# Latent attention's output projection and memory attention worked in two halves of the tokens

## The chip, the cores and the metric

The kernel runs on one core of a Trainium2 chip. The metric is the device time of one execution in microseconds (us). TensorE (PE in the rows) does the matmuls, VectorE (DVE), ScalarE (ACT) and GpSimd (POOL) do the rest, and SyncE (SP) issues the loads.

## The reference, cut to what matters

A first block is followed by two layers of a second block, for 512 tokens of width 1024. In each layer x is the residual stream:

```
x = x + 0.5 * swiglu(rms_norm(x, ffn1_norm), ...)
... three mixers: latent attention, windowed attention, neighbourhood attention
x = x + concat(rms_norm(o_mla), rms_norm(o_swa), rms_norm(o_na)) @ w_mix_out
h = rms_norm(x, mem_norm_x);  m = rms_norm(mem, mem_norm_m)
q = rms_norm((h @ w_q).reshape(512, 4, 64), q_gain)
k, v = split(m @ w_kv);  k = rms_norm(k.reshape(256, 4, 64), k_gain)
p = softmax(q @ k.T * 64 ** -0.5)      # 512 tokens x 256 memory rows, per head
x = x + (p @ v) @ w_o
x = x + 0.5 * swiglu(rms_norm(x, ffn2_norm), ...)
x = rms_norm(x, block_norm)
```

The change lies in the four lines from the projection of o_mla to w_o, in both layers.

## The kernel before, in words

x is held turned: eight tiles X(0) to X(7) of 128 features by 512 tokens. A weight matrix is loaded raw, and ScalarE and VectorE split it into a high and a low part (`chunk3`, L361 and L362); activations are split likewise (`split`, L371 to L375), and a product takes three matmuls for each 128 rows of contraction: high by high, high by low, low by high (`gemm_f`, L383 to L385, features out; `gemm_t`, L406 to L408, tokens out). There are four pairs of split weight buffers (`p_w`), two raw ones, nine `h` tiles, and in PSUM three `acc`, two `ss` and three `st` banks.

`mixer` ends with `out_proj("mla")` (L1625): for each of the eight d, 12 matmuls of 512 columns into an `ss` bank, then an addition to X(d) (L1634). `memory` (L1687) follows:

- `norm_split` scales and splits each X(k) into x (L374, L375), squares it on ScalarE (L483) and adds the squares up on GpSimd (L488). `norm.cols` sums over the features with one-column matmuls (L429) and takes the root on GpSimd (L420).
- The queries of token tile i are 24 matmuls of 256 columns. `query` (L1700) scales them by the norm (L1702), norms each head (`head_norm`, L1313 to L1316, its root at L420), and `place` (L1695) turns them (L413) and splits them into qT. The `later` and `tick` calls set by how many steps a piece of work is put off.
- `Attn` with `per=2` works in eight items, two heads of one token tile each (heads h and h + 2): `scores` (six matmuls of 64 rows by 256 columns into one `ss` bank, L1133 to L1135; maximum, L1145; exponential, L1148), `turn` (four transposes and a copy, L1183) and `values` (eight matmuls of 64 columns, L1200; division by the sum, L1213). `piped` runs scores two steps ahead of turn and three ahead of values.
- `turned` turns and splits the result, and `out(0)` and `out(1)` project it for tokens 0 to 255 and 256 to 511 (48 matmuls of 256 columns each, additions at L1735). `out(0)` runs in the background of the attention, `out(1)` at the end.

Then `norm_split` and `ffn` for ffn2 begin. The kernel is written in one stream, and every engine's queue is fixed when it is built: the framework (`TileContext(nc, schedule_with_timeline_sim=True)`) goes through the stream with a model of its own, and lets an instruction that it holds ready go ahead of one that it holds waiting. So the order on an engine is near that of the stream, and not the same. On the chip each queue is strictly in order.

Of the kernel before, what the change touches and what calls it, by code (L numbers as in the profile page):

```python
# [8 lines left out]
F32 = mybir.dt.float32  # L9
F32R = mybir.dt.float32r  # L10
# [29 lines left out]
def _chunks(w, width):  # L40
    return np.stack([_ktile(w[:, i:i + width]) for i in range(0, w.shape[1], width)])
# [87 lines left out]
def prep(I):  # L129
# [76 lines left out]
    for l in range(L2):  # L206
        for n in ("ffn1", "ffn2"):
            w = I[f"{n}_w_in_2"][l]
            w = np.concatenate([w[:, :FF].reshape(D, NFF, 128), w[:, FF:].reshape(D, NFF, 128)], axis=2).reshape(D, -1)
            A[f"{n}_a{l}"] = _chunks(w, 256)  # L210
            w = I[f"{n}_w_out_2"][l]
            A[f"{n}_b{l}"] = np.concatenate([_chunks(w[:FF // 2], 128), _chunks(w[FF // 2:], 128)])
        w = I["w_mix_in_2"][l]
        A[f"mixq{l}"] = _ktile(w[:, :256])
        A[f"mixkv{l}"] = _ktile(w[:, 256:384])
        sq = w[:, 416:672].reshape(D, 4, 64)[:, [0, 2, 1, 3]].reshape(D, 256)
        za = np.concatenate([w[:, 384:416], sq, w[:, 672:928]], axis=1)
# [9 lines left out]
        A[f"memq{l}"] = _chunks(I["mem_w_q_2"][l], 256)  # L227
        A[f"memkv{l}"] = _chunks(I["mem_w_kv_2"][l], 256)
# [9 lines left out]
class Prog:  # L238
# [104 lines left out]
        return self.p_s.tile([128, 32], F32, name="s", tag="s", bufs=17)[:, :n]  # L343


    def chunk3(self, ap, k, parts=1, low=None):

        nc = self.nc
        low = low or nc.vector
        c = ap.shape[1] // k  # L350
        per = k if k * c <= CH // 2 else -(-k // 2)
        hi, lo = [], []
        for k0 in range(0, k, per):
            m = min(per, k - k0) * c
            h = self.p_w.tile([128, CH // 2], F32R, name="wh", tag="wh")
            l = self.p_w.tile([128, CH // 2], F32R, name="wl", tag="wl")
# [149 lines left out]
def nat(i):  # L506
    return lambda t: t[:, i * 128:(i + 1) * 128]
# [24 lines left out]
def v3(t):  # L532
    return t.rearrange("p (h i) -> p h i", h=4)
# [560 lines left out]
class Attn:  # L1094
# [22 lines left out]
    def scores(self, a, b):  # L1117
        g, nc = self.g, self.g.nc
        i, h = self.tile_head(a, b)
        n_in = 4 if self.by_head else self.nh  # L1120
        lo, hi = self.window(i)
        n = hi - lo
        if b == 0:
            self.st[a] = g.small(32)
            self.bt = self.bias(i) if self.bias else None
        m, w, per = self.st[a], n * 128, self.per
        s = g.ss()[:, :per * w]
        for j in range(per):
            sj = s[:, j * w:(j + 1) * w]
            q, k = self.qT(h + j * self.step, i), self.kT(h + j * self.step)  # L1130
            if isinstance(q, tuple):
                k = [t[:, lo * 128:hi * 128] for t in k]
                nc.tensor.matmul(sj, q[0], k[0], start=True, stop=False)  # L1133
                nc.tensor.matmul(sj, q[0], k[1], start=False, stop=False)
                nc.tensor.matmul(sj, q[1], k[0], start=False, stop=True)  # L1135
            else:
                nc.tensor.matmul(v3(sj), q, k[:, lo:hi], start=True, stop=True)
        P = g.p()
        mx, l = (m[:, o + b:o + b + (per - 1) * self.step + 1:self.step] for o in (0, n_in))
        if self.bt:  # L1140
            nc.vector.tensor_tensor_reduce(P[:, :w], s, self.bt(h, lo, hi), -1.0,
                                           self.sink[:, h:h + 1] if self.sink is not None else 3e38, OP.add, OP.min, mx)
            nc.scalar.activation(P[:, :w], P[:, :w], AF.Exp, scale=-1.0, bias=mx, accum_out=l)
        else:
            nc.vector.tensor_reduce(mx, s.rearrange("p (j k) -> p j k", j=per) if per > 1 else s, axis=AX.X, op=OP.max, negate=True)  # L1145
            for j in range(per):
                c = slice(j * w, (j + 1) * w)
                nc.scalar.activation(P[:, c], s[:, c], AF.Exp, bias=mx[:, j:j + 1], accum_out=l[:, j:j + 1])  # L1148
        self.st[a, b] = P

    def scores2(self, i, h0, h1):
# [236 lines left out]
def mixer(g, l, xt, c2):  # L1388
# [298 lines left out]
def memory(g, l, xt, mem):  # L1687
    nc, A = g.nc, g.A
    X = tview(xt)
    norm = g.norm_split(X, g.c(f"mem_norm_x{l}"))  # L1690
    wh, wl = g.chunk3(A[f"memq{l}"][0], 8)
    qT = g.h(F32R)
    gq = gain_col(g, "mem", l, 0.125)

    def place(i, z):  # L1695
        ps = g.st()
# [3 lines left out]
    def query(i, ps):  # L1700
        z = g.b()[:, :256]
        nc.scalar.activation(z, ps[:, :256], AF.Copy, scale=norm.cols()[:, i:i + 1])  # L1702
        head_norm(g, z, 4, 64)
        g.later(2, place, i, z)


    pss = [g.acc() for i in range(3)]
    for ks in (range(6), range(6, KD)):
        for i in range(3):
            g.gemm_t(pss[i][:, :256], norm.parts, nat(i), wh, wl, 0, 256, ks)  # L1710
            if ks[-1] == KD - 1:
                query(i, pss[i])
                g.tick()
    half = lambda t, hb: t[hb * 64:hb * 64 + 64]
    o = g.h()
    hi, lo = g.h(F32R), g.h(F32R)
    w = {}

    def turned(i):
        ps = g.st()  # L1720
        g.turn(ps, lambda c: o[:, i, hs(c)], 2)
        kv = ps[:, :256].rearrange("p (k t) -> p k t", k=2)
        g.split(kv, hi[:, 0:2, hs(i)], lo[:, 0:2, hs(i)])
        if i == 1:
            g.bg.append(out(0))

    def out(hf):
        if not w:
            w["o"] = g.chunk3(A[f"memo{l}"], 2)
        c = slice(hf * 256, hf * 256 + 256)  # L1730
        parts = [(hi[:, k, c], lo[:, k, c]) for k in range(2)]
        for k in range(KD):
            ps = g.acc()[:, :256]
            g.gemm_f(ps, *w["o"], k * 128, k * 128 + 128, parts)
            nc.vector.tensor_tensor(X(k)[:, c], X(k)[:, c], ps, op=OP.add)  # L1735
            yield

    at = Attn(g, 4, 64, lambda h, i: tuple(half(qT[:, c + h // 2, hs(i)], h % 2) for c in (0, 2)),
              lambda h: [half(t[:, (h // 2) * 256:(h // 2) * 256 + 256], h % 2) for t in mem.kT],
              lambda t, h: mem.v[:, t * 256 + h * 64:t * 256 + h * 64 + 64], lambda i: o[:, i, :256],  # L1740
              lambda i: (0, 2), None, None, lambda i: g.later(1, turned, i), per=2)
    ps = g.ss()
    g.gemm_t(ps[:, :256], norm.parts, nat(3), wh, wl, 0, 256)
    query(3, ps)
    g.tick()
    g.pipe(at.items(), steps=2)
    g.flush()
    for _ in out(1):
        pass
# [38 lines left out]
def second_block(g, xt):  # L1788
# [5 lines left out]
    x, row = norm.parts, norm.row  # L1794
    for l in range(L2):
        ffn(g, "ffn1", l, xt, x, row)
        mem = mixer(g, l, xt, c2)
        memory(g, l, xt, mem)
# [49 lines left out]
```

## Time and profile before

| | us |
|---|---|
| median of 3 runs | 2894.86 |
| lowest and highest of them | 2879.66, 4008.79 |
| profiled execution | 2895.25 |
| its span | 2893.5 |
| TensorE busy in it | 2827.5 |
| VectorE, ScalarE, GpSimd busy | 1458.4, 1162.8, 464.0 |

The profiled execution's time is 1.75 us above its span, and 0.39 us above the median. The highest run stands alone. A matmul's start-to-start distance to the next, and not the duration in its row, says what it takes of TensorE's time, since matmuls overlap.

### The profile page before, as it was taken

How to read it: one execution, taken by the hardware profiler on the slowest of the kernel's cores; microseconds unless marked ns; L12 is line 12 of the kernel's file. 1: busy time of each engine (PE TensorE's matmuls, PEld its weight loads, DVE VectorE, ACT ScalarE, POOL GpSimd, SP SyncE). 2: the span in 40 equal slices, each digit the busy share in tenths (PEclk: the TensorE clock that was granted, in tenths of full speed). 3: DMA queues.
4: the chain of work that ended last, by engine and by line, in shares of the span. 5: the costliest groups of instructions: out<-in, count | busy, mean ns of one | idle time of the engine just before them, and what ended most of it. 6: DMA issues, size and time to landing. Idle time of an engine off the chain costs nothing.

```text
span 2893.5 us, 37993 instructions
## 1 busy us (share of the span) xinstructions
PE 2827.5 (98%) x15101; PEld 2399.4 (83%) x15101; DVE 1458.4 (50%) x2338; ACT 1162.8 (40%) x2008; POOL 464.0 (16%) x557
## 2 busy tenths in 40 slices
PE   8999999999999999999999999999999899999998
PEld 6798999888888888778888888888888778888887
DVE  5734455445434444677643444534444676644442
ACT  5323444533322235765432234322335765332232
POOL 4422222002000013512200003000013512200001
PEclk9999999999999999999799999999999999799999
DMA  4111222233323232212133323233232212133322
GB/s 154 52 45 59 74 73 74 73 103 122 99 87 105 86 106 75 68 37 66 38 102 90 107 88 108 88 85 112 84 107 70 63 40 72 31 102 90 107 88 80
DMA packets 78322, 239.63 MB, mean 83 GB/s; under 512 B 8512, under 2 KB 14656, under 8 KB 78016
## 3 DMA queue, kind: packets, MB, share of 16 engines
q1 hardware_dynamic: 78144, 237.20, 26.0%
q8 instruction: 119, 1.95, 0.3%
q14 instruction: 59, 0.48, 0.1%
HBM read 235.06 MB, written 2.10 MB: 82 GB/s over the span
## 4 chain that ended last, share of the span: by engine, by line
PE 91%; DVE 4%; ACT 2%; POOL 1%; issue 1%; DMA 0%; DVEq 0%; SPq 0%; ACTq 0%; POOLq 0%
PE ss L383 12%; PE ss L384 12%; PE ss L385 12%; PE acc L383 8%; PE acc L385 8%; PE acc L384 8%; PE acc L406 4%; PE acc L408 4%; PE acc L407 4%; PE st L413 3%; PE acc L1200 2%; PE ss L1236 2%; DVE b L611 1%; PE acc L396 1%; PE acc L395 1%; PE acc L397 1%
## 5 line engine op out<-in xcount | busy, mean ns | idle before, releaser
L362 DVE TENSOR_TENSOR wl<-raw,wh 128x1024 fp32r<-128x1024 f32 (+3 forms) x447 | 506.9, 1134 | 558.9 <-ACT wh L361 558.0
L361 ACT ACTIVATE wh<-raw 128x1024 fp32r<-128x1024 f32 (+3 forms) x459 | 449.9, 980 | 731.8 <-PE ss L384 533.7
L383 PE MATMUL acc<-x,wh 128*128 128x512 f32 x1048 | 412.7, 394 | 8.4 <-ACT wh L361 8.1
L385 PE MATMUL acc<-x,wl 128*128 128x512 f32 x1048 | 413.4, 394 | 0.1
L384 PE MATMUL acc<-x,wh 128*128 128x512 f32 x1048 | 411.3, 393 | 0.0
L383 PE MATMUL ss<-h,wh 128*128 128x512 f32 (+1 forms) x843 | 328.7, 390 | 0.0
L385 PE MATMUL ss<-h,wl 128*128 128x512 f32 (+1 forms) x843 | 326.1, 388 | 0.0
L384 PE MATMUL ss<-h,wh 128*128 128x512 f32 (+1 forms) x843 | 326.0, 388 | 0.0
L488 POOL TENSOR_TENSOR b<-b 128x512 f32<-128x512 f32 (+1 forms) x77 | 106.6, 1385 | 1176.6 <-ACT b L483 1068.6
L383 PE MATMUL ss<-x,wh 128*128 128x512 f32 x672 | 261.5, 389 | 0.1
L385 PE MATMUL ss<-x,wl 128*128 128x512 f32 x672 | 261.4, 389 | 0.0
L384 PE MATMUL ss<-x,wh 128*128 128x512 f32 x672 | 261.4, 389 | 0.0
L406 PE MATMUL acc<-wh,x 128*128 128x256 f32 (+1 forms) x880 | 252.8, 288 | 0.0
L407 PE MATMUL acc<-wl,x 128*128 128x256 f32 (+1 forms) x880 | 252.6, 288 | 0.0
L383 PEld LDWEIGHTS acc<-x,wh 128*128 128x128 f32 x1048 | 198.1, 189 | 50.8 <-ACT wh L361 8.5
L385 PEld LDWEIGHTS acc<-x,wl 128*128 128x128 f32 x1048 | 197.9, 189 | 42.6 <-DVE wl L362 1.6
L408 PE MATMUL acc<-wh,x 128*128 128x256 f32 (+1 forms) x816 | 232.1, 286 | 0.0
L384 PEld LDWEIGHTS acc<-x,wh 128*128 128x128 f32 x1048 | 197.9, 189 | 41.1 <-DVE x L375 0.6
L383 PEld LDWEIGHTS ss<-h,wh 128*128 128x128 f32 x843 | 159.3, 189 | 33.1 <-issue 0.6
L385 PEld LDWEIGHTS ss<-h,wl 128*128 128x128 f32 x843 | 159.5, 189 | 32.4
L384 PEld LDWEIGHTS ss<-h,wh 128*128 128x128 f32 x843 | 159.5, 189 | 31.6 <-issue 0.5
L1077 ACT ACTIVATE b<-b 128x512 f32<-128x512 f32 x88 | 55.6, 632 | 310.0 <-DVE b L1076 309.9
(384 smaller groups left out, 4813.6 us busy)
## 6 DMA issues: line engine op xcount, KB each, us to landing
raw<-in_ffn_a SPq DMA_DIRECT2D x176, 512.0 KB, 3.7
raw<-in_ffn_b SPq DMA_DIRECT2D x64, 384.0 KB, 3.1
raw<-in_ffn_b SPq DMA_DIRECT2D x64, 320.0 KB, 2.9
raw<-in_w_swa SPq DMA_DIRECT2D x36, 512.0 KB, 3.9
raw<-in_w_gate SPq DMA_DIRECT2D x16, 512.0 KB, 3.8
raw<-in_w_qkv SPq DMA_DIRECT2D x12, 512.0 KB, 3.9
raw<-in_mixN SPq DMA_DIRECT2D x12, 512.0 KB, 3.8
raw<-in_mixA SPq DMA_DIRECT2D x8, 544.0 KB, 3.7
```

Of the source, the lines that this page charges most:

```text
L361: nc.scalar.activation(h[:, s], r[:, s], AF.Copy)
L362: low.tensor_tensor(l[:, s], r[:, s], h[:, s].bitcast(F32), op=OP.subtract)
L383: mm(ps, a, xh, start=first and k == 0, stop=False)
L384: mm(ps, a, xl, start=False, stop=False)
L385: mm(ps, b, xh, start=False, stop=last and k == n - 1)
L406: mm(ps, a, wh[k][:, c0:c1], start=k == 0, stop=False, **part)
L407: mm(ps, a, wl[k][:, c0:c1], start=False, stop=False, **part)
L408: mm(ps, b, wh[k][:, c0:c1], start=False, stop=k == n - 1, **part)
L413: self.nc.tensor.transpose(ps[:, i * 128:(i + 1) * 128], src(i), self.ident)
L488: (engine or nc.gpsimd).tensor_tensor(acc, acc, sq, op=OP.add)
L1200: nc.tensor.matmul(self.pso[:, c:c + d], PT[:, hs(j * n + k)], self.v(lo + k, hj), start=k == 0, stop=k == n - 1)
L1236: nc.tensor.matmul(v3(s), self.q[h // 4][:96, i, hs(h % 4)], self.k[h // 4][:96, :, hs(h % 4)], start=True, stop=True)
```

## The change

`mixer` no longer runs the projection of o_mla; it hands its parts to `memory`, which splits the 512 tokens in halves of 256.

- `residual(hf, d)` does the projection, the addition, the split and the square of one d for one half. The four chunks of w_mix_out are all split beforehand and serve both halves; the first half uses the `ss` banks, the second `acc`.
- `products` and `queries` replace the norm's columns and `query`: a half's two token tiles are squared, copied, and scaled together, with one root for the norm and one for the heads.
- The heads of w_q and w_k are reordered on the host, so that the two heads of an item lie on partitions 0 to 63 and 64 to 127. `scores` gives each head an `ss` bank of its own, alternates their matmuls, and takes one maximum for each.
- w_q is split into two `h` tiles instead of the weight buffers.
- The order is written out: all eight d of the first half and two of the second, the first half's queries, the other six d with the first half's attention between them, the second half's queries with more of it, then `out(0)`, the second half's attention, and `out(1)`.

```diff
@@ chunk3
-    def chunk3(self, ap, k, parts=1, low=None):
+    def chunk3(self, ap, k, parts=1, low=None, into=None):
...
+            if into:
+                h, l = (t.rearrange("p a b -> p (a b)")[:, k0 * c:k0 * c + m] for t in into)
+            else:
...
@@ Attn.scores
-        s = g.ss()[:, :per * w]
...
+        ss = [g.ss()[:, :w] for j in range(per)]
+        qk = [(self.qT(h + j * self.step, i), self.kT(h + j * self.step)) for j in range(per)]
+        for qi, ki in ((0, 0), (0, 1), (1, 0)):
+            for s, (q, k) in zip(ss, qk):
+                nc.tensor.matmul(s, q[qi], k[ki][:, lo * 128:hi * 128], start=qi + ki == 0, stop=qi == 1)
...
-            nc.vector.tensor_reduce(mx, s.rearrange("p (j k) -> p j k", j=per) if per > 1 else s, axis=AX.X, op=OP.max, negate=True)
...
+            for j, s in enumerate(ss):
+                nc.vector.tensor_reduce(mx[:, j:j + 1], s, axis=AX.X, op=OP.max, negate=True)
+                nc.scalar.activation(P[:, j * w:(j + 1) * w], s, AF.Exp, bias=mx[:, j:j + 1], accum_out=l[:, j:j + 1])
@@ mixer, memory
-    for _ in out_proj("mla"):
-        pass
-    return mem
...
+    wo = [g.chunk3(A[f"mixo_mla{l}"][m], 4) for m in range(4)]
+    wqh, wql = g.chunk3(A[f"memq{l}"][0], 8, into=wq)
...
+    def residual(hf, d):
+        c = hh[hf]
+        ps = (g.acc if hf else g.ss)()[:, c]
+        g.gemm_f(ps, *wo[d // 2], d % 2 * 128, d % 2 * 128 + 128, [(a[:, c], b[:, c]) for a, b in mla])
+        nc.vector.tensor_tensor(X(d)[:, c], X(d)[:, c], ps, op=OP.add)
+        g.split(X(d)[:, c], x[d][0][:, c], x[d][1][:, c], gain[:, d:d + 1])
+        sq = g.b()[:, :256]
+        nc.scalar.activation(sq, X(d)[:, c], AF.Square)
...
+            nc.gpsimd.tensor_tensor(acc[hf], acc[hf], sq, op=OP.add)
...
+    def queries(hf):
+        rc = rcs[hf]
+        g.rsqrt(rc[:, 0:2], g.col_sums(acc[hf], [nat(0), nat(1)]), 1.0 / D)
+        nc.vector.tensor_tensor(rc[:, 2:4], rc[:, 0:2], rc[:, 0:2], op=OP.mult)
+        m = g.small(16)
+        for n in range(2):
+            i = 2 * hf + n
+            z, sq = g.b()[:, :256], g.b()[:, :256]
+            nc.scalar.activation(sq, zs[i][:, :256], AF.Square)
+            nc.scalar.activation(z, zs[i][:, :256], AF.Copy)
...
+        g.rsqrt(m[:, 8:16], m[:, 0:8], 1.0 / 64)
...
+    first, second = g.piped(items[:4]), g.piped(items[4:])
+
+    def step(it):
+        next(it, None)
+        g.tick(0)
+
+    for d in range(KD):
+        residual(0, d)
+    for d in range(2):
+        residual(1, d)
+    for i in (0, 1):
+        products(i, range(KD))
+    queries(0)
+    for d in (2, 3):
+        residual(1, d)
+    for n, d in enumerate(range(4, KD)):
+        if n < 2:
+            place(n)
+        residual(1, d)
+        if n >= 1:
+            step(first)
+    for ks in (range(6), range(6, KD)):
+        for i in (2, 3):
+            products(i, ks)
+            step(first)
+    queries(1)
+    o0 = out(0)
+    for n in range(4):
+        step(first)
+        if n:
+            next(o0, None)
+    for i in (2, 3):
+        place(i)
+        next(o0, None)
+    for n in range(7):
+        step(second)
+        next(o0, None)
     g.flush()
     for _ in out(1):
         pass
```

## Rows read from the trace of the kernel before

**Rows 1.** The page, busy time of each engine in the span.

```profile
PE 2827.5 (98%) x15101; PEld 2399.4 (83%) x15101; DVE 1458.4 (50%) x2338; ACT 1162.8 (40%) x2008; POOL 464.0 (16%) x557
```

**Rows 2.** Windows: length, busy us (instructions) by engine, PE clock, DMA share, GB/s.

```profile
1345.70:1380.80 35.10, 35.08 (x206) 30.81 (x204) 23.07 (x30) 18.02 (x27) 12.92 (x9) 1.00 0.29 90
...
1385.50:1415.00 29.50, 28.96 (x137) 24.94 (x137) 14.78 (x30) 10.18 (x38) 2.38 (x3) 0.53 0.03 11
1415.00:1431.00 16.00, 15.53 (x127) 15.05 (x127) 10.78 (x22) 5.90 (x11) 2.54 (x2) 1.00 0.00 1
2467.90:2502.20 34.30, 33.63 (x152) 29.63 (x153) 16.06 (x34) 10.18 (x38) 2.40 (x3) 0.50 0.03 11
2428.10:2516.50 88.40, 82.56 (x467) 73.80 (x466) 53.09 (x92) 37.96 (x86) 19.54 (x15) 0.81 0.15 49
```

**Rows 3.** Waits of TensorE: total us, times, longest.

```profile
PE st L413 <- DVE s L419: 9.6, 2, 4.8
```

**Rows 4.** Timeline of TensorE in the projection and the queries, layer 0.

```profile
1347.12 0.39 PE L385 MATMUL ss<-h,wl 128*128 128x512 f32 x1
1347.35 0.39 PE L383 MATMUL ss<-h,wh 128*128 128x512 f32 x1
...
1357.26 0.40 PE L406 MATMUL acc<-wh,x 128*128 128x256 f32 x2
...
1374.57 0.28 PE L408 MATMUL acc<-wh,x 128*128 128x256 f32 x1
1374.69 0.28 PE L406 MATMUL acc<-wh,x 128*128 128x256 f32 x1
```

**Rows 5.** Timeline of TensorE in the memory attention, layer 0.

```profile
1413.48 1.89 PE L1200 MATMUL acc<-b,pt 128*128 128x64 f32 x16
1415.18 0.36 PE L384 MATMUL acc<-h,wh 128*128 128x256 f32 x1
...
1417.39 0.60 PE L413 MATMUL st<-cst,p 128*128 128x128 f32 x4
1417.74 0.36 PE L383 MATMUL acc<-h,wh 128*128 128x256 f32 x1
```

**Rows 6.** Timeline of TensorE: windowed attention's scores, two heads alternating in two banks.

```profile
1178.95 0.62 PE L1164 MATMUL ss<-h 64*128 64x256 f32 x6
1179.50 0.50 PE L383 MATMUL acc<-x,wh 128*128 128x512 f32 x1
```

**Rows 7.** VectorE by line, 1345.7 to 1361: busy us, mean ns, then idle.

```profile
L362 DVE TENSOR_TENSOR wl<-raw,wh 128x1024 fp32r<-128x1024 f32 x4 | 5.2, 1304 | 0.3 <-ACT wh L361 0.2
L375 DVE SCALAR_TENSOR_TENSOR x<-h,cst,x 128x512 fp32r<-128x512 f32 x4 | 3.9, 1004 | 0.8 <-ACT x L374 0.8
```

**Rows 8.** VectorE by line, 1380 to 1431.

```profile
L1735 DVE TENSOR_TENSOR h<-h,acc 128x256 f32<-128x256 f32 x14 | 5.9, 419 | 3.1 <-PE acc L385 2.9
L1183 DVE COPY pt<-st 128x512 f32<-128x512 f32 x8 | 5.5, 689 | 3.6 <-PE st L413 3.6
...
L375 DVE SCALAR_TENSOR_TENSOR h<-st,s,h 128x256 fp32r<-128x256 f32 x4 | 1.9, 481 | 1.4 <-ACT h L374 1.4
...
L1314 DVE TENSOR_REDUCE s<-b 128x4 f32<-128x256 f32 x4 | 1.6, 413 | 0.1
```

**Rows 9.** ScalarE by line, 1380 to 1431.

```profile
L1148 ACT ACTIVATE p<-ss,s 128x256 f32<-128x256 f32 x16 | 7.5, 474 | 8.3 <-DVE s L1145 8.3
```

**Rows 10.** GpSimd by line, 1345 to 1431.

```profile
L488 POOL TENSOR_TENSOR b<-b 128x512 f32<-128x512 f32 x9 | 13.3, 1475 | 59.1 <-issue 48.5 <-ACT b L483 10.6
L420 POOL TENSOR_TENSOR s<-s,half 128x4 f32<-128x4 f32 x4 | 3.9, 1008 | 3.5 <-DVE s L419 3.5
```

**Rows 11.** Timeline of TensorE at the end of neighbourhood attention, layer 0.

```profile
1233.36 1.09 PE L1554 MATMUL st<-cst,b 128*96 128x128 f32 x4 [1.60 <-DVE b L1602]
```

**Rows 12.** Windows: the 10 us around that wait.

```profile
1230.00:1240.00 10.00, 8.19 (x35) 6.97 (x35) 4.78 (x17) 2.53 (x8) 4.18 (x5) 0.66 0.16 52
```

**Rows 13.** ScalarE's weight splits, 1335 to 1385: ns min/median/max, first and last start.

```profile
L361 ACT ACTIVATE wh<-raw x10: 1042/1054/1064, 1337.9 to 1380.8; 128x1024 fp32r<-128x1024 f32 x10
```

More of the change, by code (lines that the diff above doesn't have):

```diff
@@ L226, in prep @@
         A[f"mixo_na{l}"] = _chunks(w[768:], 512)
-        A[f"memq{l}"] = _chunks(I["mem_w_q_2"][l], 256)
-        A[f"memkv{l}"] = _chunks(I["mem_w_kv_2"][l], 256)
+        order = lambda w: w.reshape(D, 4, 64)[:, [0, 2, 1, 3]].reshape(D, 256)
+        A[f"memq{l}"] = _chunks(order(I["mem_w_q_2"][l]), 256)
+        w = I["mem_w_kv_2"][l]
+        A[f"memkv{l}"] = _chunks(np.concatenate([order(w[:, :256]), w[:, 256:]], axis=1), 256)
         A[f"memo{l}"] = _ktile(I["mem_w_o_2"][l])
@@ L354, in chunk3 @@
             m = min(per, k - k0) * c
-            h = self.p_w.tile([128, CH // 2], F32R, name="wh", tag="wh")
-            l = self.p_w.tile([128, CH // 2], F32R, name="wl", tag="wl")
+            if into:
+                h, l = (t.rearrange("p a b -> p (a b)")[:, k0 * c:k0 * c + m] for t in into)
+            else:
+                h = self.p_w.tile([128, CH // 2], F32R, name="wh", tag="wh")
+                l = self.p_w.tile([128, CH // 2], F32R, name="wl", tag="wl")
             r = self.p_raw.tile([128, CH // 2], F32, name="raw", tag="raw")
@@ L1126, in scores @@
         m, w, per = self.st[a], n * 128, self.per
-        s = g.ss()[:, :per * w]
[L1128 to L1137, printed above, removed]
+        ss = [g.ss()[:, :w] for j in range(per)]
[3 more added lines that the diff above has]
+                nc.tensor.matmul(s, q[qi], k[ki][:, lo * 128:hi * 128], start=qi + ki == 0, stop=qi == 1)
         P = g.p()
@@ L1681, in mixer, with memory, products, place @@
     g.flush()
-    for _ in out_proj("mla"):
-        pass
-    return mem
-def memory(g, l, xt, mem):
+    return mem, parts["mla"]
+def memory(g, l, xt, mem, mla):
     nc, A = g.nc, g.A
     X = tview(xt)
-    norm = g.norm_split(X, g.c(f"mem_norm_x{l}"))
-    wh, wl = g.chunk3(A[f"memq{l}"][0], 8)
-    qT = g.h(F32R)
-    gq = gain_col(g, "mem", l, 0.125)
-    def place(i, z):
-        ps = g.st()
+    gain = g.c(f"mem_norm_x{l}")
+    wo = [g.chunk3(A[f"mixo_mla{l}"][m], 4) for m in range(4)]
+    hh = [slice(0, 256), slice(256, 512)]
+    wq = g.h(F32R), g.h(F32R)
+    wqh, wql = g.chunk3(A[f"memq{l}"][0], 8, into=wq)
+    xh, xl = [g.x4(), g.x4()], [g.x4(), g.x4()]
+    x = [(xh[k // 4][:, k % 4], xl[k // 4][:, k % 4]) for k in range(KD)]
+    qT, o, hl = g.h(F32R), g.h(), g.h(F32R)
+    gq = gain_col(g, "mem", l, 0.125)
+    acc = [None, None]
+    rcs = [g.p_s.tile([128, 8], F32, name="rc", tag="rc", bufs=3) for _ in range(2)]
+    def residual(hf, d):
[6 more added lines that the diff above has]
+        nc.scalar.activation(sq, X(d)[:, c], AF.Square)
+        if acc[hf] is None:
+            acc[hf] = sq
+        else:
+            nc.gpsimd.tensor_tensor(acc[hf], acc[hf], sq, op=OP.add)
+    zs = {}
+    def products(i, ks):
+        if ks[0] == 0:
+            zs[i] = g.acc()
+        g.gemm_t(zs[i][:, :256], x, nat(i), wqh, wql, 0, 256, ks)
+    def queries(hf):
[8 more added lines that the diff above has]
+            nc.scalar.activation(z, zs[i][:, :256], AF.Copy)
+            zs[i] = z
+            nc.vector.reduce_sum(m[:, 4 * n:4 * n + 4], sq.rearrange("p (h d) -> p h d", h=4), axis=AX.X)
+            nc.vector.tensor_scalar(m[:, 4 * n:4 * n + 4], m[:, 4 * n:4 * n + 4], rc[:, 2 + n:3 + n], None, op0=OP.mult)
+        g.rsqrt(m[:, 8:16], m[:, 0:8], 1.0 / 64)
+        for n in range(2):
+            zv = zs[2 * hf + n].rearrange("p (h d) -> p h d", h=4)
+            f = m[:, 8 + 4 * n:12 + 4 * n]
+            nc.vector.tensor_scalar(f, f, rc[:, n:n + 1], None, op0=OP.mult)
+            nc.vector.tensor_tensor(zv, zv, bc(f, 64), op=OP.mult)
+    def place(i):
+        z, ps = zs.pop(i), g.st()
@@ L1697, in place @@
         g.turn(ps, lambda hp: z[:, hs(hp)], 2)
         g.split(ps[:, :256].rearrange("p (k t) -> p k t", k=2), qT[:, :2, hs(i)], qT[:, 2:, hs(i)], gq)
[L1700 to L1713, printed above, removed]
@@ L1714, in memory @@
     half = lambda t, hb: t[hb * 64:hb * 64 + 64]
-    o = g.h()
-    hi, lo = g.h(F32R), g.h(F32R)
     w = {}
@@ L1721, in turned @@
         g.turn(ps, lambda c: o[:, i, hs(c)], 2)
[L1722 to L1725, printed above, removed]
+        g.split(ps[:, :256].rearrange("p (k t) -> p k t", k=2), hl[:, 0:2, hs(i)], hl[:, 2:4, hs(i)])
     def out(hf):
[L1728 to L1731, printed above, removed]
+        c = hh[hf]
@@ L1732, in out @@
         for k in range(KD):
+            if not w:
+                w["o"] = g.chunk3(A[f"memo{l}"], 2)
             ps = g.acc()[:, :256]
-            g.gemm_f(ps, *w["o"], k * 128, k * 128 + 128, parts)
+            g.gemm_f(ps, *w["o"], k * 128, k * 128 + 128, [(hl[:, n, c], hl[:, 2 + n, c]) for n in range(2)])
             nc.vector.tensor_tensor(X(k)[:, c], X(k)[:, c], ps, op=OP.add)
             yield
-    at = Attn(g, 4, 64, lambda h, i: tuple(half(qT[:, c + h // 2, hs(i)], h % 2) for c in (0, 2)),
-              lambda h: [half(t[:, (h // 2) * 256:(h // 2) * 256 + 256], h % 2) for t in mem.kT],
+    at = Attn(g, 4, 64, lambda h, i: tuple(half(qT[:, c + h % 2, hs(i)], h // 2) for c in (0, 2)),
+              lambda h: [half(t[:, (h % 2) * 256:(h % 2) * 256 + 256], h // 2) for t in mem.kT],
@@ L1740, in memory @@
               lambda t, h: mem.v[:, t * 256 + h * 64:t * 256 + h * 64 + 64], lambda i: o[:, i, :256],
               lambda i: (0, 2), None, None, lambda i: g.later(1, turned, i), per=2)
[L1742 to L1746, printed above, removed]
+    items = at.items()
+    first, second = g.piped(items[:4]), g.piped(items[4:])
[4 more added lines that the diff above has]
+        residual(0, d)
@@ L1796, in second_block @@
         ffn(g, "ffn1", l, xt, x, row)
-        mem = mixer(g, l, xt, c2)
-        memory(g, l, xt, mem)
+        memory(g, l, xt, *mixer(g, l, xt, c2))
         norm = g.norm_split(X, g.c(f"ffn2_norm{l}"))
```

5 lines of the change are left out of this document (1 added, 4 removed).

## The prediction

> **What bounds the kernel now.** I read the page's busy times first: TensorE is busy 2827.5 us of 2893.5 [rows 1], so only what shortens TensorE's queue counts. But busy is not full speed, so next I read the windows around the change, and there the clock column [rows 2]. In layer 0 the stage from the projection's first matmul to the last of `out(1)` takes 1345.7 to 1431.0, 85.3 us; in layer 1 it takes 88.4. The mean is 86.9, of which four or five matmuls of ffn2 take about 1, so 86. Its first 35.1 us (projection and queries) run at clock 1.00 with TensorE never idle. Then comes an idle stretch of 4.7 us, and after it the attention, with TensorE busy 28.96 of 29.5 us at 0.53, and in layer 1 33.63 of 34.3 at 0.50: the lower of the clock's two levels, 1.2 and 2.4 GHz. The idle stretch is one wait of 4.8 us in each layer [rows 3]: the first transposes of queries wait for the head norms. So the stage has two losses, the wait and the half clock after it: 29.5 x 0.47 = 13.9 us in layer 0 and 34.3 x 0.50 = 17.2 in layer 1, 15.5 on average.
>
> **The change part by part.** All sums are per layer, at full clock, and start to start.
>
> *Projection in halves.* 96 matmuls of 512 columns at 0.23 (22.1 us) become 192 of 256 columns at 0.12 (23.0) [rows 4]: +0.9, on the path. The other engines get twice the instructions at more than half the time each, and that lies beside TensorE, with one exception below.
>
> *Queries and output.* Each keeps its 96 matmuls of 256 columns: 96 x 0.12 = 11.5, twice [rows 4].
>
> *Values and transposes.* Values keep 64 matmuls at 1.70 / 16 = 0.106: 6.8. Transposes (8 for the queries, 32 for the items, 8 for the results) take 0.35 / 4 = 0.09 each: 4.2 [rows 5]. The eight one-column sums I put at a transpose's 0.09 each: 0.7, an estimate.
>
> *Scores.* The six matmuls of an item stood in one bank; now two heads alternate in two. Six such matmuls of the windowed attention take 0.55 us, 0.092 each [rows 6], where 256 columns by themselves take 0.12 [rows 4]. So 48 x 0.092 = 4.4 in place of 5.8. The Trainium skill ("TensorEngine Tiling (Array Packing)", Theoretical Speedup) lets two 64-row matmuls run up to twice as fast together; by that the six would take 0.36 and the layer 2.9 us, 3 us less over both layers. This trace shows 1.3 times, so I stay with its row.
>
> Together 23.0 + 11.5 + 11.5 + 6.8 + 4.2 + 0.7 + 4.4 = 62.1 us of TensorE. The stage before, by the same prices, is 22.1 + 11.5 + 11.5 + 6.8 + 4.2 + 0.7 + 5.8 = 62.6; with 4.8 of wait and 15.5 of half clock that makes 82.9, and 3 of its 86 are small waits. So nothing is won by less work. Everything hangs on how much of the 23.4 us of losses goes, and on the new ones:
>
> *The first half's projection* runs out of VectorE. A d has 1.44 us of TensorE (12 x 0.12). VectorE has an addition of 0.42 [rows 8] and a split, which with GpSimd running beside it took 1.00 for 512 columns, so about 0.5. Over eight d that is 7.4 us, and four weight splits of 1.30 lie in the same stretch [rows 7]: 12.6 against 11.5 of TensorE. The two d of the second half (2.9 us) cover the difference, but with only two `ss` banks some waits will show. I take 2 us; the ends are 0 (the framework fills them with later d) and 4.
>
> *The first half's query chain* (squares, roots, scaling, transposes) cost the 4.8 us. It had four roots of 1.0 us in series on GpSimd [rows 10]; now there is one for two tiles, after one for the norm. It lies beside six d of the second half, 8.6 us, and the first half's four items lie beside three of these d and the 5.8 us of second queries. I put both at nothing. With that cover gone the 4.8 are back.
>
> *The second half's query chain* lies beside `out(0)` (48 x 0.12 = 5.8), which needs the first half finished; again nothing.
>
> *The second half's attention* then has nothing left beside it. Its chain: place, a transpose pair and two splits of 0.48, 1.2 together; per item scores 0.55, the first maximum 0.41 (priced by a reduction of the same 256 columns [rows 8]) and two exponentials of 0.47 [rows 9]. Two `ss` banks mean that the next item's scores wait for these, so an item takes 1.9, with hand-overs some 2.1. The Trainium skill speaks of the same price (same page, Gotcha 1: row tiles write different PSUM banks, so bank pressure rises); no row here shows it for this attention. Four items: 8.4. After the last: transposes 0.35, copy 0.69, values 0.86, division 0.6, turned and split 1.0: 3.5. In all 1.2 + 8.4 + 3.5 = 13.1, in which TensorE has 4 x (0.55 + 0.35 + 0.85) + 0.7 = 7.7 of work. New wait: 5.4 us. At the low end it is 1 (part of `out(0)` is left to fill it), at the high end 7.
>
> *The clock.* In that stretch TensorE waits in pieces, the longest at the end. A wait of 1.60 us at the end of neighbourhood attention [rows 11] stands in ten microseconds at 0.66 [rows 12]: 10 x 0.34 = 3.4 us lost. I charge one such fall: 3.4. The low end is 0; the high end has all of the second attention and `out(1)` at half clock, about 8.
>
> *Queues moved past.* SP: w_q's two loads move behind w_mix_out's four and no longer wait for a weight buffer, as its split goes into `h` tiles; w_o's loads wait for the first two chunks of w_mix_out, free when the second half's d = 3 is done, 30 us ahead of need; ffn2's first chunk waits for the other two, free after d = 7. ScalarE's first splits start at 1337.9, before the projection does [rows 13]; a chunk now serves two d in 2.9 us and not 5.5, while a split takes 1.05 on ScalarE and 1.30 on VectorE, so the first half's supply just holds. If it doesn't, each late chunk costs some 2 us, and that is within the 4 above. GpSimd gets 14 additions of 256 columns for 7 of 512 (1.48 each [rows 10]); between 0.74 and 1.48 each, that is 10 to 21 us in 23 of projection. Only the last of each half is waited for, by the norm's sums, and the queries' matmuls stand between. Host reordering costs nothing on the chip.
>
> Sum: 62.1 + 2 + 5.4 + 3.4 = 72.9 against 86: 13.1 saved per layer, 26 in the kernel. The profiled execution took 2895.25, 0.39 above the median of the runs shown, so I forecast 2869 us.
>
> **The rivals.**
>
> *All hidden.* The framework lets ready matmuls go ahead: query matmuls of `memory` already stand between two d of the projection, at 1357.26 [rows 4]. If it saves enough of `out(0)` for the second attention, the new wait is 1 and the clock holds: 62.1 + 2 + 1 = 65.1, 21 saved twice, 2853. For it: six d and two query tiles are free to move. Against it: work that is ready is taken early, and `out(0)` stands ahead in the stream.
>
> *The queues undo the order.* The same freedom, with a model that errs, may put a waiting instruction in front. Then 4.8 us of query wait return, with four items (7.7) at half clock, and with the second attention's losses as above the stage takes 62.1 + 2 + 4.8 + 7.7 + 5.4 + 1 = 83: 3 saved per layer, 2889. For it: the framework's model is not the chip. Against it: in the projection of before TensorE never waits [rows 2].
>
> *Half clock all the way* ends on the slow side. In the stage of before the clock, once fallen, stayed down for some 30 us though TensorE was busy all the time, and rose only with the dense matmuls of `out` [rows 2]. If a wait before the first attention brings it down, and the mixture of attention and projections doesn't bring it back before `out(1)` ends, then 4.3 (three d) + 5.8 (queries) + 11.5 (out) + about 15 of attention, 36.8 us, run at half clock: 62.1 + 2 + 36.8 = 100.9, 15 more than before, 2925 in all. It decides from 22 us of work at half clock (86 - 64.1). Against it: the fall among neighbourhood attention and projections cost no more than 3.4 us [rows 12].
>
> **How the numbers follow.** The forecast has 0.64, all hidden 0.14, undone order 0.13, half clock all the way 0.05, and 0.04 is left for what I don't see. The forecast's own ends: 62.1 + 0 + 4 + 0 saves 20, and 62.1 + 3 + 6 + 7 saves 8 per layer, so 2855 to 2879. With "all hidden" at 2853 and 5 us for the difference between runs of the same kernel (two of those shown lie 15 apart) the low end is 2848. The high end takes in the undone order, 2890. A measurement of this kernel tells about 2% from no change, 58 us. All losses of both layers together are 47, so faster by over 2% has 0.02; slower by over 2% needs 29 us per layer, beyond even the third rival: 0.02; within 2%: 0.96.
>
> **What would show each step right or wrong.** In the trace after: no wait of 4.8 us before queries are turned; clock 1.00 from the projection to the end of the first attention; six scores in 0.55 us; projection matmuls 0.12 apart; TensorE waits of together some 5 us in the second attention, the longest ahead of `out(1)`; and a stage of 73 us. I am wrong if the first attention runs at 0.50, if TensorE waits for VectorE's additions in the first eight d by more than 4 us, or if the second attention is filled with projections.

## The result, and the profile after

The changed kernel takes 2916.94 us (median of 5 runs, 2912.24 to 2918.26) against 2895.03 before: a ratio of 1.0084, 95% interval 1.0058 to 1.0111. I had forecast 26 us less; it is 22 us more, outside my range on the slow side. The profiled execution took 2918.26 us with a span of 2916.4.

The windows of layer 0's stage after, and the whole stage of layer 1 (columns as in [rows 2]):

```profile
1347.00:1381.10 34.10, 32.25 (x270) 32.05 (x268) 30.03 (x55) 21.99 (x47) 16.34 (x16) 1.00 0.34 109
1384.00:1397.00 13.00, 11.89 (x46) 9.42 (x46) 4.25 (x10) 3.94 (x14) 0.00 (x0) 0.50 0.00 0
1398.00:1418.00 20.00, 17.09 (x127) 14.77 (x128) 12.68 (x36) 5.54 (x18) 2.34 (x2) 1.00 0.00 1
1418.50:1438.00 19.50, 17.73 (x76) 15.84 (x77) 6.94 (x15) 5.31 (x15) 0.15 (x1) 0.50 0.00 1
1347.00:1442.70 95.70, 87.14 (x565) 78.65 (x564) 61.22 (x126) 42.28 (x103) 24.64 (x23) 0.82 0.14 45
2443.50:2542.30 98.80, 89.80 (x565) 80.71 (x564) 61.19 (x125) 41.95 (x102) 25.86 (x22) 0.81 0.14 43
```

Read the clock column downwards: where before had one stretch at the low level [rows 2], there are now two, one in each half's attention, with full clock during `out(0)` between them. The stage is longer by 10.6 us in layer 0 (95.7 against 85.1) and by 10.7 in layer 1 (98.8 against 88.1), and that is nearly all of the loss; the 1000 us between the stages add 3.5 in this execution, but three kernels below that don't have the change (`e5`, `e12`, `e13`) show 4.2 to 4.7 there too.

The waits of TensorE in layer 0's stage after:

```profile
PE st L418 <- DVE b L1739: 2.4, 2, 1.9
PE ss L1136 <- ACT p L1146: 2.2, 2, 1.1
PE acc L1198 <- DVE pt L1181: 1.6, 2, 0.8
PE st L418 <- DVE h L1211: 1.0, 2, 0.5
PE acc L388 <- ACT h L376: 0.5, 1, 0.5
PE acc L413 <- DVE x L380: 0.4, 1, 0.4
PE ss L1136 <- ACT h L379: 0.3, 1, 0.3
```

The one wait of 4.8 us [rows 3] has become eleven smaller ones, 8.4 us in all (8.7 in layer 1), where the stage of before had 5.8. L418 turns queries, probabilities and results, L1136 is a score, L1198 a value.

Where the cover went is seen in TensorE's lines of the first 34 us (busy us, mean ns, idle):

```profile
L388 PE MATMUL ss<-h,wh 128*128 128x256 f32 x32 | 9.1, 286 | 0.0
...
L388 PE MATMUL acc<-h,wh 128*128 128x256 f32 x32 | 9.0, 285 | 0.0
L412 PE MATMUL acc<-h,x 128*128 128x256 f32 x23 | 6.3, 283 | 0.0
```

`ss` holds the first half's projection and `acc` the second's. All 32 first products of either (4 for each of eight d) are done before the first queries are turned at 1381.13, and 23 of the 32 query products (L412) too. None of the six d that stand behind `queries(0)` in the stream is left for the first attention: three had been pulled forward, in among the first half's d, and three stand under the query chain. Why the framework put them there no run shows. The chain itself, as VectorE, ScalarE and GpSimd run it:

```profile
1372.35 0.38 ACT L1729 ACTIVATE b<-acc 128x256 f32<-128x256 f32 x1 [0.69 <-PE acc L413]
...
1375.02 0.57 DVE L424 TENSOR_SCALAR s<-s 128x8 f32<-128x8 f32 x1
...
1375.50 1.21 DVE L367 TENSOR_TENSOR wl<-raw,wh 128x1024 fp32r<-128x1024 f32 x1
1375.67 2.55 POOL L425 TENSOR_TENSOR s<-s,half 128x8 f32<-128x8 f32 x1
...
1379.00 1.21 DVE L367 TENSOR_TENSOR wl<-raw,wh 128x1024 fp32r<-128x1024 f32 x1
1380.14 1.81 DVE L1739 TENSOR_TENSOR b<-b,s 128x256 f32<-128x256 f32 x2
```

From the squares to the turn it lasts 8.8 us. One root of the heads (L425) is left, of 2.55 us, where four took 1.0 each [rows 10], and VectorE's queue has two weight splits (L367) and the second half's additions inside the chain. Under it lay only three d and 20 query matmuls, 6.7 us; so TensorE ran dry for 1.9. What was left for the first attention was 28 query products: four around its first scores, and 24 only from its first values on.

In layer 1 no wait before the first attention is above 1.1 us, and that attention stands at the low level all the same:

```profile
2477.99 0.44 PE L418 MATMUL st<-cst,b 128*128 128x128 f32 x2 [0.31 <-DVE b L1739]
2478.99 0.50 PE L1136 MATMUL ss<-b,h 64*128 64x256 f32 x4 [0.56 <-ACT h L379]
2480.61 0.41 PE L418 MATMUL st<-cst,b 128*128 128x128 f32 x2 [1.11 <-DVE b L1739]
```

```profile
2482.00:2499.50 17.50, 16.39 (x65) 13.52 (x64) 6.01 (x15) 4.85 (x18) 0.00 (x0) 0.53 0.03 13
```

### The profile page after: what moved, and what is told of

Same layout as the page of the kernel before. It is cut to its first block, busy times and chain, and to the rows that moved or that the text cites. A ratio compares the mean times of both kernels' runs of the same rounds, so it can differ in the third digit from the quotient of the medians.

```text
span 2916.4 us, 38496 instructions
## 1 busy us (share of the span) xinstructions
PE 2846.4 (98%) x15293; PEld 2418.1 (83%) x15293; DVE 1469.9 (50%) x2404; ACT 1169.0 (40%) x2040; POOL 468.5 (16%) x569
## 4 chain that ended last, share of the span: by engine, by line
PE 90%; DVE 4%; ACT 3%; POOL 1%; issue 1%; DMA 0%; DVEq 0%; SPq 0%; ACTq 0%; POOLq 0%
PE ss L388 12%; PE ss L390 12%; PE ss L389 12%; PE acc L388 8%; PE acc L389 8%; PE acc L390 8%; PE acc L411 4%; PE acc L413 4%; PE acc L412 4%; PE st L418 3%; PE acc L1198 2%; PE ss L1234 2%; DVE b L616 1%; PE acc L400 1%; PE acc L402 1%; PE acc L401 1%
## 5 line engine op out<-in xcount | busy, mean ns | idle before, releaser
L367 DVE TENSOR_TENSOR wl<-raw,wh 128x1024 fp32r<-128x1024 f32 (+3 forms) x443 | 501.4, 1132 | 562.6 <-ACT wh L366 561.9
L388 PE MATMUL ss<-h,wh 128*128 128x512 f32 (+1 forms) x843 | 321.4, 381 | 1.1 <-DVE h L1704 1.1
L389 PE MATMUL ss<-h,wh 128*128 128x512 f32 (+1 forms) x843 | 318.6, 380 | 0.1
L390 PE MATMUL ss<-h,wl 128*128 128x512 f32 (+1 forms) x843 | 318.4, 379 | 0.0
L493 POOL TENSOR_TENSOR b<-b 128x512 f32<-128x512 f32 (+1 forms) x63 | 84.8, 1347 | 1114.0 <-ACT b L488 1106.3
L411 PE MATMUL acc<-wh,x 128*128 128x256 f32 (+1 forms) x832 | 239.9, 288 | 0.0
L412 PE MATMUL acc<-wl,x 128*128 128x256 f32 (+1 forms) x832 | 239.7, 288 | 0.0
L413 PE MATMUL acc<-wh,x 128*128 128x256 f32 (+1 forms) x768 | 219.6, 286 | 0.0
```

The costliest lines, as they stand in the source:

```text
L388: mm(ps, a, xh, start=first and k == 0, stop=False)
L389: mm(ps, a, xl, start=False, stop=False)
L390: mm(ps, b, xh, start=False, stop=last and k == n - 1)
L411: mm(ps, a, wh[k][:, c0:c1], start=k == 0, stop=False, **part)
L412: mm(ps, a, wl[k][:, c0:c1], start=False, stop=False, **part)
L413: mm(ps, b, wh[k][:, c0:c1], start=False, stop=k == n - 1, **part)
```

## The experiments

Theory 1: the order written was undone and the cover used up, so both attentions stand bare; their waits bring the clock down. Theory 2: the two PSUM banks per item cost the time. Each kernel was timed against the kernel before in the same session (its medians were 2894.0, 2893.6, 2891.8 and 2893.9). Stage lengths and clocks are of the profiled execution, layer 0 and layer 1. There is one such execution of each kernel, and the clock differs from execution to execution; where a reading leans on it, the mean clock over all of a kernel's executions is given too.

| kernel | median us | ratio, 95% | stages us | clock in them |
|---|---|---|---|---|
| before | 2895.0 | | 85.1, 88.1 | 0.82, 0.81 |
| changed | 2916.9 | 1.0058 to 1.0111 | 95.7, 98.8 | 0.82, 0.81 |
| e1_one_bank | 2903.0 | 1.0025 to 1.0076 | 86.9, 86.1 | 0.90, 0.92 |
| e2_pairs_alone | 2904.7 | 1.0032 to 1.0080 | 91.8, 93.1 | 0.78, 0.78 |
| e3_cover | 2904.3 | 1.0034 to 1.0084 | 92.8, 92.7 | 0.83, 0.87 |
| e4_cover_one_bank | 2892.9 | 0.9994 to 1.0040 | 90.4, 82.2 | 0.85, 0.96 |
| e5_fill_wait | 2881.2 | 0.9928 to 0.9996 | 80.5, 74.8 | 0.92, 1.00 |
| e6_order_held | 2888.9 | 0.9972 to 1.0001 | 82.7, 87.5 | 0.94, 0.90 |
| e7_order_two_banks | 2894.8 | 0.9999 to 1.0029 | 86.3, 88.3 | 0.92, 0.92 |
| e8_fill_after | 2906.8 | 1.0030 to 1.0065 | 93.7, 96.7 | 0.85, 0.84 |
| e9_fill_both | 2899.4 | 1.0011 to 1.0038 | 88.9, 89.7 | 0.92, 0.94 |
| e10_cover_fill | 2894.0 | 0.9988 to 1.0018 | 86.1, 82.6 | 0.90, 0.98 |
| e11_chain_first | 2885.0 | 0.9969 to 1.0018 | 82.7, 81.6 | 0.86, 0.85 |
| e12_splits_last | 2883.2 | 0.9960 to 0.9997 | 77.0, 79.9 | 0.91, 0.89 |
| e13_splits_last_fill | 2888.1 | 0.9969 to 1.0009 | 84.4, 84.2 | 0.82, 0.82 |

**Banks and order, apart and together.** `e1_one_bank` takes the two banks out of the change (scores, head order and head pairing as before):

```diff
-ss = [g.ss()[:, :w] for j in range(per)]
+s = g.ss()[:, :per * w]
```

> The changed kernel, but with the two heads of an item in one PSUM bank and heads paired as in the kernel before. Theory 1 (the cover was used up: the second half's projection runs before the first query chain is done, so both attentions stand bare and their waits bring the clock down): the two waits and the two stretches at half clock stay; only the 1.1 us waits of scores for exponentials go, some 2 to 4 us per layer, so 2909 to 2915. Theory 2 (the two banks per item make the scores wait and run head by head, and this costs the time): the 22 us go away, 2890 to 2897.

`e2_pairs_alone` puts the same lines, the other way round, into the kernel before.

> The kernel before, with nothing of the change but the head order and two PSUM banks per item in the scores. Theory 1: the wait of 4.8 us for the head norms and the half clock after it stay as they are; 2892 to 2900. Theory 2: most of the loss is here, 2907 to 2917.

`e3_cover` ties the second half's d behind the queries (instructions traced in the block stand behind the named one in its engine's queue; `g.last` is TensorE's last product or transpose):

```diff
+with g.tc.issue_after(g.last.ins):
     queries(0)
     for d in (2, 3):
         residual(1, d)
...
     if n < 2:
         place(n)
+    with g.tc.issue_after(g.last.ins):
         residual(1, d)
```

> The changed kernel, with the second half's d = 2 to 7 tied behind the first half's query matmuls and the transposes of queries on TensorE, so that they can't be run early. Theory 1: no wait over 1 us before the first attention, its stretch at full clock, the second attention bare as it was; about 14 us less of half clock and wait per layer at most, 5 at least, less 2 us of new waits while VectorE feeds the first half: 2893 to 2908. Theory 2: the waits of scores stay, 2913 to 2920.

`e4_cover_one_bank` has both edits.

> Both: the second half's d tied behind the queries, and one PSUM bank per item. Theory 1: as with the tie alone, less 2 to 4 us per layer: 2886 to 2902. Theory 2: as with one bank alone, 2890 to 2897, the tie adding nothing.

The four answers make a square. From two banks to one: 13.9 us less without the tie (2916.9 to 2903.0), 11.4 with it (2904.3 to 2892.9), and 10.7 between `e2` and the kernel before. From no tie to the tie: 12.6 less with two banks, 10.1 with one. The executions of `e1` alone spread over 24 us, so such a difference is known to some 5 us. `e1` and `e2` fell between the ranges of the two theories, `e3` into that of theory 1, `e4` into both. So each theory is right about half of the loss, neither about the whole, and together they only bring the change back to where it started.

What the banks do is seen in TensorE's timeline of the second attention, in the changed kernel:

```profile
1412.95 0.91 PE L1136 MATMUL ss<-b,h 64*128 64x256 f32 x6 [0.35 <-ACT h L379]
1414.97 0.62 PE L1136 MATMUL ss<-b,h 64*128 64x256 f32 x3 [1.11 <-ACT p L1146]
1415.52 0.44 PE L418 MATMUL st<-cst,p 128*128 128x128 f32 x2
1415.88 0.61 PE L1136 MATMUL ss<-b,h 64*128 64x256 f32 x3
1416.43 0.44 PE L418 MATMUL st<-cst,p 128*128 128x128 f32 x2
```

and in `e1_one_bank`:

```profile
1416.14 0.38 PE L1136 MATMUL ss<-b,h 64*128 64x256 f32 x1
1416.36 0.28 PE L1137 MATMUL ss<-b,h 64*128 64x256 f32 x1
...
1416.83 0.28 PE L1138 MATMUL ss<-b,h 64*128 64x256 f32 x1
1417.04 0.66 PE L416 MATMUL st<-cst,p 128*128 128x128 f32 x4
```

In this attention only the first item has its six scores together. The next waits 1.11 us for an exponential to free a bank, and from there on the two heads go one by one: three matmuls in 0.55 us, two transposes, three in 0.55. That is 1.1 for the six, where one bank takes 0.90 (1416.14 to 1417.04) and I had put 0.55. Three matmuls of one head take as long as six in pairs did in the windowed attention [rows 6]; the pairing that was to make scores quicker hardly takes place.

The tie didn't clear the first wait either. In `e3_cover` it is

```profile
PE st L418 <- DVE b L1739: 3.8, 1, 3.8
```

for only two d (2.9 us) stand between the queries and their turning, under a chain of 7.2 us (1364.03 to 1371.19). That is the order as written: between `queries(0)` and the first `place` it has d = 2 and 3 and no more, so what the framework had put there (6.7 us) was more cover than this. And the next two d, dense work, stand at the low level behind the wait:

```profile
1371.10:1377.20 6.10, 6.01 (x28) 5.94 (x28) 2.16 (x6) 1.65 (x4) 0.73 (x1) 0.51 0.23 76
```

So a wait of 3.8 us does bring the clock down. Whether it takes such a wait is asked below.

**The order held throughout.** `e6_order_held` has one bank, four d under the first query chain, then one dense piece behind each step of the first attention, and `out(0)` half under the second chain, half between the second attention's items; `e7_order_two_banks` is the same with two banks.

```diff
+chunks = [(residual, 1, 6), (residual, 1, 7)] + [(products, i, ks)
+          for i in (2, 3) for ks in (range(4), range(4, KD))]
+for f, *a in chunks:
+    step(first)
+    with g.tc.issue_after(g.last.ins):
+        f(*a)
```

> The changed kernel with one PSUM bank per item and the order tied on TensorE: four d of the second half cover the first query chain, the other two and the second half's query products stand in pieces between the first attention's items, half of out(0) covers the second query chain and the other half stands between the second attention's items. If cover is what was missing, no wait over 1.5 us and at most one short fall of the clock: stage 70 to 76 us, 2860 to 2875. If the mixture of attention and projections brings the clock down by itself, it is no better than the last run with the tie and one bank: 2886 to 2896.

> The same tied order, with the change's two PSUM banks per item. If the banks cost by themselves, 8 to 12 us more than the tied order with one bank. If they cost only where the attention stands bare (waits that bring the clock down), within 3 us of it.

The stages of `e6` stand at clock 0.94 and 0.90, so (1 - 0.94) x 82.7 = 5.0 and 8.8 us of half clock, against 15.3 and 16.7 before and 17.2 and 18.8 in the changed kernel: with dense work that really stands between the items half to two thirds of it goes. `e7`, with the change's banks, has 6.9 and 7.1, and the median of the mean clocks is 0.988 in both, against 0.981 before and 0.977 in the changed kernel. Yet the stage is 82.7 and 87.5, far from the 70 to 76 expected, and the kernel's 2888.9 lies in the range of the second answer. The first answer's condition wasn't met: waits of 1.5 to 1.8 us are left, and all waits are 7.3 and 8.8 us. Two banks cost 5.9 more here, less than elsewhere but over the 3 that would have made them harmless.

**Fillers in the waits.** To price wait and clock, matmuls whose result nothing reads were put into the waits: `e5_fill_wait` in the kernel before, `e8_fill_after` and `e9_fill_both` in the changed one, `e10_cover_fill` in `e4`. The edits move a little order too: `e5` puts off the turning of the queries (`later` 4 in place of 2), and in `e8` and `e9` all of the second half's d stand ahead of the fillers and `place` behind them.

```diff
+ws = g.st()
+with g.tc.issue_after(g.last.ins):
+    for _ in range(20):
+        last = nc.tensor.matmul(ws, norm.parts[0][0][:, :128], norm.parts[1][0], start=True, stop=True)
+with g.tc.issue_after(last.ins):
     g.tick()
```

> The kernel before, with work added: 20 matmuls of 512 columns per layer whose result nothing reads, placed in the wait of 4.8 us before the queries are turned (20 x 0.23 = 4.6 us). If the idle stretch brings the clock down, the attention after it runs at full clock and about 15 us per layer are saved: 2862 to 2872. If the attention's own thin work brings it down, the fall comes all the same, later: 2886 to 2897.

> The changed kernel, with work added: 16 matmuls of 256 columns per layer whose result nothing reads, behind the second half's last d, in the wait of 1.9 us before the first queries are turned (16 x 0.12 = 1.9 us). If this wait brings the clock down, the first of the two stretches at half clock goes, 5 to 8 us per layer: 2901 to 2908. If the first attention's own work does it, nothing changes: 2913 to 2921.

> The changed kernel, with work added whose result nothing reads: the 16 matmuls before the first queries are turned, and five groups of 6 matmuls of 256 columns tied behind pieces of out(0) and of the second attention (30 x 0.12 = 3.6 us per layer; the second attention waits 3.2 us without them). If the second stretch at half clock comes from these waits and thin pieces, it goes, and its price of some 8 us per layer with it, beyond what the fillers cost: 2888 to 2898, against 2907 with the first fillers alone. If not, the fillers cost their time: 2907 to 2914.

> The changed kernel with one bank per item and the tie (2893 before), with work added whose result nothing reads: 30 matmuls of 256 columns (3.7 us) per layer in the wait of 3.8 us before the first queries are turned. Stage at full clock: 69 of work, 2.3 of ffn2's matmuls, 3.8 of fillers, 3.6 of other waits: 79. If the wait brings the clock down, the stage comes near that in both layers: 2872 to 2884, and so not below the kernel before with fillers (2881). If not, 2888 to 2897.

`e5` gains 12 us, less than the 22 to 32 expected if the wait alone brought the clock down. Its two layers say why (windows of the attention in layer 0, and of the attention and `out` in layer 1):

```profile
1390.00:1403.00 13.00, 13.00 (x60) 11.34 (x59) 5.96 (x12) 4.34 (x18) 0.00 (x0) 0.50 0.00 0
2463.00:2503.20 40.20, 37.49 (x284) 33.40 (x283) 29.33 (x63) 20.14 (x59) 6.43 (x7) 1.00 0.09 27
```

The same code ran with the same small waits (1.0, 0.6 and 0.2 us in both layers), once at half clock for 13 us in which TensorE was never idle, once not at all.

`e8` is 10.1 us below the changed kernel, which is in the range of theory 1; but in the profiled executions only 4.1 of 11.4 us lie in the two stages (95.7 to 93.7 and 98.8 to 96.7), and the rest lies outside, where the edit does nothing. So the hit is in part luck. `e9` gains another 7.4, a little less than expected, and its stages are 11.8 us shorter together: the stretches at half clock are shorter and not all gone.

`e10` gains nothing over `e4` and lies in the range for "the wait does not". But where `e4` had the low level behind its wait of 3.8 us, `e10` in its profiled execution, at 2883.8 us the lowest of its twelve, holds full clock from the filled wait on, through the first attention with its d between the items:

```profile
1365.00:1385.00 20.00, 18.67 (x143) 17.09 (x142) 14.09 (x28) 10.74 (x27) 5.73 (x6) 1.00 0.25 79
2450.00:2470.00 20.00, 18.67 (x143) 17.09 (x142) 14.26 (x26) 10.90 (x28) 5.49 (x6) 1.00 0.26 79
```

What is left at the low level there is the second attention and `out(1)`.

**The wait removed by queue order.** In the kernel before, the column sums stood in TensorE's queue 2.0 us after GpSimd had the sums, and weight splits stood inside the query chain. `e11_chain_first` changes these queues, `e12_splits_last` holds the splits longer, `e13_splits_last_fill` adds six fillers.

```diff
+with g.tc.issue_after(g.sums.ins):
     g.gemm_t(*a)
...
+a, b = self.hold
+with self.tc.issue_after(a), self.tc.issue_after(b):
+    return self.chunk3_(ap, k, parts, low)
```

The last 30 products of the queries stand behind the sums, weight splits behind `hold`: in `e11` the last head norm, in `e12` the split of the last query tile.

> The kernel before, nothing of the change and no work added or left out; only the order of its queues near the query chain is changed: the norm's column sums stand ahead of 30 query matmuls of TensorE (they waited 2.0 us in its queue behind query matmuls, though GpSimd had the sums), ffn2's and w_o's weight splits stand behind the query chain on ScalarE and VectorE (three of 1.05 and three of 1.23 us stood inside it), and queries of tiles 1 to 3 are turned behind the first scores. The wait of 4.8 us should shrink to about 1. If the wait brings the clock down, the half clock goes too, 15 per layer: 2856 to 2868. If the attention's own thin work does, only the wait is saved: 2880 to 2888.

> As the run before (the kernel before with the column sums ahead of 30 query matmuls and the query chain ahead of the weight splits; no work added or left out), but the weight splits of w_o and ffn2 stand behind the split of the last query tile: there they held up the first scores by 1.8 and 1.2 us, and the clock fell at that point in both layers. If those waits brought it down, the clock holds for most of the attention: 2858 to 2872. If the attention's thin work is enough, some 3 us of waits per layer go and the half clock stays: 2876 to 2885.

> The same, with work added whose result nothing reads: 6 matmuls of 512 columns (1.4 us) per layer in the wait of about 1.1 us left before the first queries are turned. If waits bring the clock down, 2855 to 2868, whatever is left of half clock gone. If the thin work does, within 4 us of the run without fillers.

`e12` does what was meant to the waits (those of 1374 to 1386, and the windows before, in and after the attention):

```profile
PE st L421 <- DVE s L427: 1.1, 1, 1.1
PE ss L1141 <- ACT h L381: 0.6, 1, 0.6
PE st L421 <- ACT p L1156: 0.2, 1, 0.2
```

```profile
1378.00:1385.00 7.00, 5.31 (x40) 4.39 (x38) 4.54 (x14) 4.14 (x10) 4.37 (x5) 1.00 0.00 1
1385.00:1399.00 14.00, 13.79 (x62) 11.50 (x61) 10.04 (x17) 8.39 (x23) 0.00 (x0) 0.54 0.23 76
```

The 4.8 us are 1.1, and the attention still falls to half clock, in both layers, for less long: (1 - 0.91) x 77.0 = 6.9 and 8.8 us of it, against 15.3 and 16.7 before. Over all executions the clock hardly moved (median of the means 0.983, against 0.981 before), and `e11` and `e12` both lie in the range for "only the wait is saved". `e13` fills that wait too; it is 4.9 us above `e12` and far from the 2855 to 2868 of the other answer, and in layer 1:

```profile
2473.50:2504.00 30.50, 30.50 (x145) 28.10 (x146) 17.30 (x32) 12.21 (x38) 0.00 (x0) 0.51 0.22 69
```

30 us at half clock, TensorE busy in all of them, after waits of 1.0 and 0.6. So a long wait brings the clock down (`e3`), but is not needed for the fall, and theory 1's second half (waits bring the clock down) is not the whole of it. Waits of up to 1.1 us are left in all of these kernels; whether they start the fall isn't shown, and in `e5` the same ones did in one layer and not in the other. What these stretches share is the attention itself: small transposes, scores and values, with 21 of `out(0)`'s products among the 145 instructions of the last one. The Trainium skill ("TensorE: Matmul & The Clock Gate", A second HAM failure mode: psum-queue depth-cycling) tells of such a case, where TensorE idles very briefly between groups of matmuls and its clock goes up and down. Here the profile shows no idle time in the stretch, only the low level, so whether the same is at work is open. `e5_fill_wait` and `e12_splits_last` are below the kernel before, by 0.04 to 0.72% and 0.03 to 0.40%; `e12` does it with no work added.

## Why the prediction was wrong

The stages are 21 and 24 us above the 73 forecast, once the 1.6 us of ffn2's products that stand in them are taken off. Roughly 14 and 15 of that are half clock, 6 and 7 are work of TensorE, and 1 to 2 are waits. Against the kernel before the half clock is only some 2 us more per layer: it is why nothing was won, and the loss itself lies in the waits and in the work.

- **The clock** is the term that failed most: "I charge one such fall: 3.4". Measured, (1 - 0.82) x 95.7 = 17 us in layer 0 and 19 in layer 1, more than before's 15 and 17. I had tied the half clock to the 4.8 us wait and taken it as gone with the wait, and as price of a new one the fall at a single 1.6 us wait among dense projections [rows 11, 12]. Layer 1 of the changed kernel, `e5`, `e12` and `e13` show that the bare attention goes to half clock with no wait above 1.1 us before it, in most layers though not in all. What decides between the two layers of `e5` the runs don't show.
- **The query chain at nothing.** I counted six d, 8.6 us, as cover, and three of them again for the first attention. The order as written has only two d between `queries(0)` and the first `place`, and `e3`, which holds it there, waits 3.8 us. In the changed kernel the framework had moved d and query products, as "the queues undo the order" had it: three d went in among the first half's (my brackets under its projection, "fills them with later d"), where TensorE is never idle in layer 0 and for 1.1 us in layer 1, so my 2 us there are 0 and 1.1; three d and 20 query products covered the chain, and none was left for the attention. The waits before the queries are turned are 2.4 and 1.4 us in all. The chain is 8.8 us, for weight splits and additions queue inside it.
- **The first attention beside three d and the second queries** has 28 query products and no d beside it, and runs at 0.50: the first of the signs that I had named.
- **Scores, 48 x 0.092 = 4.4.** The row was of scores that go in pairs [rows 6]; these go head by head at 0.55 for three, 16 x 0.55 = 8.8, an estimate from the rows above, and two banks cost the kernel 11 to 14 us, and 6 in the held order.
- **TensorE's work of 62.1** was too low. Layer 1 of `e5` is the stage of before at full clock: 74.8, less 2.7 of waits, 4.7 of fillers and 0.9 of ffn2's products, is 66.4 against my 62.6; what I had called 3 us of small waits in the stage of before is 1.0 by its waits, and the rest is such work. Layer 1 of `e4`, one bank and nearly full clock, is 82.2 - 7.3 of waits - 3.3 of half clock - 2.3 of ffn2 = 69.3. The halves add 1.2 of that, where I had 0.9 (96 matmuls in 11.6 us, twice, against 22.0); what makes up the rest was not taken apart. So even with one bank the restructuring costs some 3 us of work per layer, an estimate from these two stages, where I had it 0.5 cheaper.
- **The second attention's wait, 5.4.** It is 0.35 + 1.11 + 0.79 + 0.52 + 0.47 = 3.2. The sum of waits, 2 + 5.4 = 7.4 forecast, 8.4 and 8.7 measured, came out near by luck: half or more of the waits measured stand where I had put nothing.
- **The rivals.** "Half clock all the way" came nearest in time (2925) and in its 36.8 us at the low level (34 and 38 measured, twice the 17 and 19), but not in its mechanism: the clock came back with `out(0)` and fell again. "Queues undo the order" had the mechanism and priced its half clock at one attention.

Of the 23.4 us of losses per layer that were to be won, the best order of the change (`e6`) wins 10.3 and 7.9 of half clock, but its stages are only 2.4 and 0.6 us shorter than those of before; waits take some 2 and 3 back, and more work the rest. The changed kernel wins none.

## What to carry to other kernels

A slow clock behind a wait is not yet the wait's doing alone: fill or shorten the wait by itself and look at the clock, over several executions, before moving work for it. Work counted as cover must be counted once, in the order as written, and held in its place, or a scheduler that lets ready work go ahead spends it earlier; and a chain that it is to cover is as long as all that stands in its engines' queues, not as the sum of its own instructions. Look first for what stands in the wrong place in the chain's queues: holding weight splits back and the sums ahead was worth more here than the whole rearrangement.

## What the runs showed of the hardware

The kernel before has a spread of its own that goes with the clock: 29 runs of one session go from 2867.58 us at a mean clock of 0.991 to 2897.69 at 0.980, with the same instructions in the same queues. 0.011 x 2893 is 32 us, and the time differs by 30. That is as much as the half clock of both attentions costs in the profiled execution (2 x 15.5); whether it is these that stay away in the executions at 0.991 no trace shows, for the one profiled was at 0.980. So the clock in the stage of a single profile is one draw of several, and differences of a few us between kernels in that band are not settled by it.

A stretch at half clock costs less than half of its length: layer 1's stage of before, 82.3 us busy of which 33 at half clock, takes 67.4 at full clock in `e5` (72.1 busy less 4.7 of fillers), so 14.9 for 33. Where the text takes (1 - clock) x length as the price of half clock, it is that much too high.

In scores of 64 rows, three matmuls of one head take 0.55 us and six of two heads in two banks take 0.55 [rows 6]: the second head costs nothing where both banks are free at the same time, and where they are not, its matmuls take 0.55 of their own.
